# Sparse attention of a two-layer decoder trunk: the order of the attention slots' work

## The chip, the cores and the metric

One NeuronCore of a Trainium2 chip runs the whole kernel. The metric is the device time of one execution in microseconds (us). Three runs of the kernel before gave 2098.74, 2096.32 and 2098.92 us. The engines are TensorE (PE: matmuls; PEld: their weight loads), VectorE (DVE), ScalarE (ACT), GpSimd (POOL), and SyncE (SP), whose queue issues nearly all DMAs. Each engine takes its instructions in the order in which the program has them.

## What is computed

Two layers over 1024 tokens of width 1024: a gated linear attention layer, then a sparse attention layer, each with a projection, a residual layer norm and a gated addition. The change lies in the second layer, whose core is

```python
score = jnp.einsum('bths,bth->bts', rel, wi_b) * INDEX_SCALE      # indexer, causal
_, idx = lax.top_k(score, topk)                                   # 256 keys for each query
logits = jnp.einsum('bthd,btjd->bthj', q_b, k_sel) * ATTN_SCALE
probs = jax.nn.softmax(logits, axis=-1)
o = jnp.einsum('bthj,btjd->bthd', probs, v_sel)                   # 16 heads of 128
return (o * jax.nn.silu(z)) @ w_out
```

The kernel doesn't gather: it finds each query's threshold score, turns it into a bias that hides all other keys, and computes dense attention over the causal keys. All matmuls run on float32 split in a high and a low part, three matmuls for one.

## The kernel before

The second layer runs in two halves of 512 queries. Half 0 has up to 512 keys, half 1 up to 1024. X, the layer's input, lies in SBUF; q and the gate z of each head, and the output projection, are made by *units*: a unit is one 128-column weight block times X (24 matmuls of 512 columns), or half the output columns for a pair of heads (24 matmuls; one for two pairs has 48). `slots()` lists which units run in which slot. There are 17 slots in a half, h = -1 to 15.

In slot h the program places, between the matmuls of the units, the attention work of two heads (`attend`):

- the scores of head h+1 (`A`, four blocks t of 128 queries): matmuls into S, on DVE the bias and the row's limit (`L1371`, into P), on ACT the exponential (`exp`), on DVE the inverse of its sum (`inverse`), then `scaled`, which multiplies and writes into the one buffer sq (on POOL in half 0, on ACT in half 1), and `turned`, a transpose of 32x32 squares on DVE ("the turns");
- the stores of head h+1 (`store`): four DMAs from sq to DRAM for each 512 keys, so 4 in half 0 and 8 in half 1;
- the loads of the turned probabilities PT (`load`): one of 1 MB for each 512 keys. In half 0 it is issued in slot h+1, in half 1 the first (PT0) at the end of slot h and the second (PT1) in slot h+1. PT has two buffers in half 0, one in half 1 for each load;
- of head h, whose PT was loaded: `parts`, which splits PT into a copy ph (ACT) and the rest (a subtraction, on POOL in half 0 and DVE in half 1), 3 groups of keys in half 0 and 7 in half 1; and `pv`, the matmuls with v into o. The last pv is followed by the gate and the split into u, which the output units read.

The order is set while the program is written out. `Flow` keeps a clock that advances by each matmul's nominal time; `at(t, f)` and `after(dt, f)` put a step on a heap, and steps that are due are written between two groups of three matmuls. A step that raises NotReady (`req`) is tried again 0.3 later. So a step's number sets its place in each engine's row, not when it runs. `spread` places a list of steps evenly. `Weights` loads each unit's weight block (wst), makes its high part whi on ACT and its low part wlo on DVE; in half 0 the low parts of the second layer's blocks are stored (wlos) and in half 1 loaded. A `Background` writes one step of a generator every so many us: `topk_steps` (the thresholds of blocks 4 to 7, through half 0: it stores three score tiles, then sets their lowest bit in place, then finds the threshold bit by bit, counting on ACT and DVE), and the residual's transposes (slots 0 to 4).

Each unit of q is followed by its rotation (`rope`: a POOL multiplication, a DVE shuffle, multiplication and addition) and a split on ACT and DVE. After slot 15 come three more output units, then the tail (norm, gate). `load_p` in slot 15 loads two tiles of p (xst) for the tail and splits them into the buffers of q.

Of the kernel before, what the change touches and what calls it, by code (L numbers as in the profile page):

```python
# [11 lines left out]
F32R = mybir.dt.float32r  # L12
# [35 lines left out]
class Flow:  # L48
# [20 lines left out]
    def after(self, dt, fn):  # L69
        self.at(self.now + dt, fn)  # L70
# [155 lines left out]
def trunk_kernel(ctx, tc, x_tok, x_T, p_T, pos, freq, g_q, g_k, g_v, g_z, g_a, g_a2, g_ba, g_gn, g_o,  # L226
# [3 lines left out]
    fl = Flow(nc)  # L230
# [46 lines left out]
    def slots():  # L277


        yield [("z", 0), ("q", 1), ("z", 1)]  # L280
        z = 2
        for h in range(16):
            units = [("q", h + 2)] if h < 14 else []
            g = h // 4 - 1
            if g < 0 or h == 6:
                n = 1 + (h == 6)
            else:
                n = 0 if h % 4 < 2 and h < 14 else 2 if h < 15 else 0
            units += [("z", z + i) for i in range(n)]
            z += n  # L290
            if h < 14 and g >= 0 and h % 4 < 2:
                units.insert(h % 4 == 0, ("o", (2 * g, 2 * g + 1), h % 4))
            yield units + ([("o", (6,), 0)] if h == 15 else [])
        assert z == 16
# [443 lines left out]
                    u["out"] = (i + 1) // 4  # L738
                yield

    def load_p(layer, half, alloc):
        P = []
        for k in range(2):
            st = xp.tile([128, HT], F32, tag="xst", name="xst", bufs=2)
            nc.sync.dma_start(st, p_T[layer, k, :, half * HT:half * HT + HT])
            ph, pl = alloc(), alloc()
            after(3.0, lambda ph=ph, pl=pl, st=st: split(ph, pl, st))
            P.append((ph, pl))
        return P

# [238 lines left out]
    def topk_steps(Ts, scs, sp, junk, tmp, on_act=()):  # L989
# [32 lines left out]
        for i, j in enumerate(on_act):  # L1022
            n = scs[j].shape[1]
            nc.sync.dma_start(sc_s[i, :, :n], scs[j])
            dve.tensor_scalar(kr[:, j:j + 1], kr0[:, j:j + 1], 2.0, -float(n), op0=OP.mult, op1=OP.add)
            yield
            yield
            si = scs[j].bitcast(I32)
            dve.tensor_scalar(si, si, 1, None, op0=OP.bitwise_or)
            yield  # L1030
# [308 lines left out]
    def attend(st, h, half, ap, sq):  # L1339
# [14 lines left out]
        def A(t):  # L1354
            def f():
# [17 lines left out]
                    lim = mx  # L1373

                def scaled():
                    fl.req(st["x"] == nb * h, ("e", h, t) in st)
                    to, rows = by_key[:, t, :n // 128], P.rearrange("p (j b r) -> p j b r", b=4, r=32)
                    if half:
                        act.activation(to, rows, AF.Copy, scale=sm)  # L1379
                    else:  # L1380
                        pool.tensor_scalar(to, rows, sm, 0.0, op0=OP.mult, op1=OP.add)
                    st["P", h, t] = True
                    after(0.5 + n / 700.0, turned)

                def turned():
                    x = squares[:, t, :, :n // 128]
# [6 lines left out]

                def inverse():
                    dve.reciprocal(sm, sm)
                    st["e", h, t] = True
                after(0.9, exp)
                fl.at(max(fl.now + 1.8 + n / 1200.0, st["slot"] + 3.5 + (0.3 + n / 1000.0) * t), scaled)
            return f

        def store(i):
# [11 lines left out]
        def load(i):  # L1413

            def f():
                dt, = get(("dram", h, i))
                fl.req(st["pv"] >= (h * G - (0 if i else G - 4) if half else (h - 1) * G))
                PT = ap.tile([128, 4, HT], F32R, tag=f"PT{i}", name="PT", bufs=2 - half)
                nc.sync.dma_start(PT.bitcast(F32), dt.rearrange("b p a c -> (b p) a c"))
                st["PT", h, i] = PT  # L1420
            return f
# [79 lines left out]
    res, st = {}, {}  # L1501
# [44 lines left out]
    for half in range(NH):  # L1546
# [11 lines left out]
        for h, units in enumerate(plan, -1):  # L1558
            start = st["slot"] = fl.now
            dur = sum(len(u[1]) if u[0] == "o" else 1 for u in units) * B + core * (1.0 if h >= 0 else 0.5)  # L1560
            if h >= 0:
                _, parts, pvs, _, loads = S[h]
                fl.at(start + (1.5 if half else 0.8), loads[half])
                lead = 9.0 if half else 7.4
                spread(parts, start + lead, dur - lead - 2.4)
                spread(pvs, start + lead + 2.9, dur - lead - 2.4)
            if h < 15:
                first, _, _, stores, loads = S[h + 1]
                spread(first, start + 0.3, 5.8 if half else 4.4)
                for i, f in enumerate(stores):  # L1570
                    fl.at(start + (11.5 if half else 8.2) + 0.5 * i, f)
                if half:
                    fl.at(start + max(dur - 1.0, 18.0), loads[0])
            if h == 15:
                Pt = load_p(1, half, lambda: small_tile("q", F32R, 4))
            if h == -1:
                rows = x2_tiles(half)
                next(rows)
            elif h == 0:
                y = xp.tile([128, 4, D], F32, tag="y", name="y")  # L1580
                bg2.set(residual(y, rows), 4.6 if half else 3.3)
            elif h == 4:
                bg2.finish()
            fl.run(*(unit(u) for u in units))
# [82 lines left out]
```

## Time and profile before

| | us |
|---|---|
| median of three runs | 2098.74 |
| profiled execution | 2106.36 |
| its span, first to last instruction | 2104.1 |
| PE busy in it | 1998.5 |
| half 0 of the attention, first scores to slot 14 | 1104.7 to 1447.0 |
| half 1, first scores to slot 14 | 1578.5 to 1979.1 |

The mean granted clock of TensorE in the span was 0.984 of full speed. A slot is counted here from the first score matmul of a head to that of the next. The busy windows of the profile give for each stretch how long each engine was busy and the clock granted in it; the waits say which instruction an engine stood idle for, and what released it. What runs beside a busy PE costs nothing by itself.

### The profile page before, as it was taken

Reading aid. Unit: us, or ns where it says so; the run is one execution under the profiler, and the core shown is the slowest. Engines: PE = TensorE matmul, PEld = TensorE weight load, DVE = VectorE, ACT = ScalarE, POOL = GpSimd, SP = SyncE. Lnnn points to the kernel's source line nnn. Section 1 sums busy time; section 2 is a strip of 40 time slices with the busy share of each in tenths; the row PEclk is TensorE's granted clock in tenths of the full one; section 3 lists DMA queues with packets and bytes.
Section 4 is the critical chain, followed back from the end, with each engine's and each line's share of the span. In section 5 each row is a group of like instructions: output and inputs, shape, how many; then the busy total and the mean of one; then the engine's idle time right before and its main releaser. Section 6 shows DMA issues by size and latency. Waiting matters only on the chain.

```text
span 2104.1 us, 26226 instructions
## 1 busy us (share of the span) xinstructions
PE 1998.5 (95%) x8984; PEld 1622.8 (77%) x8984; DVE 1496.1 (71%) x3139; ACT 1153.6 (55%) x2105; POOL 258.6 (12%) x307
## 2 busy tenths in 40 slices
PE   8999999999999999999998999998799999999979
PEld 6788888888787888888876777777577777777767
DVE  5665565676867767668599887877886676767764
ACT  5563535354565353535466677766536666666623
POOL 0110000010002010001011343432100000000000
PEclk9999999999999999999999999999999999999989
DMA  4422222224431212122454887777457876868642
GB/s 143 161 81 82 81 82 80 81 86 145 146 121 53 99 66 97 64 97 81 150 175 131 256 254 237 229 222 228 159 185 254 271 253 232 300 236 303 243 143 92
DMA packets 108021, 336.37 MB, mean 160 GB/s; under 512 B 12656, under 2 KB 13296, under 8 KB 101744
## 3 DMA queue, kind: packets, MB, share of 16 engines
q1 hardware_dynamic: 107888, 334.71, 47.6%
q8 instruction: 70, 1.15, 0.2%
q14 instruction: 63, 0.52, 0.1%
HBM read 245.73 MB, written 88.93 MB: 159 GB/s over the span
## 4 chain that ended last, share of the span: by engine, by line
PE 65%; DVE 14%; ACT 8%; DMA 6%; issue 5%; POOL 1%; SPq 1%; DVEq 0%; POOLq 0%; ACTq 0%
PE pb L58 48%; PE o L58 7%; PE U L58 6%; DVE wlo L170 2%; PE S L58 2%; ACT sq L1379 2%; DVE P L1371 1%; DMA wlo<-wlos 1%; ACT P L1391 1%; DVE sq L1387 1%; DMA PT<-sqd 1%; DVE rt L867 1%; DVE sc L980 1%; DVE tk L1002 1%; SPq L1409 1%
## 5 line engine op out<-in xcount | busy, mean ns | idle before, releaser
L58 PE MATMUL pb<-x,whi 128*128 128x512 f32 x2272 | 713.9, 395 | 5.1 <-ACT whi L166 2.4
L58 PEld LDWEIGHTS pb<-x,whi 128*128 128x128 f32 x2272 | 421.4, 190 | 83.7 <-ACT whi L166 3.2
L58 PE MATMUL pb<-x,wlo 128*128 128x512 f32 x1136 | 446.4, 393 | 0.4 <-DVE wlo L170 0.3
L166 ACT ACTIVATE whi<-wst 128x512 fp32r<-128x512 f32 x556 | 327.2, 621 | 130.0 <-PE pb L58 31.3
L170 DVE TENSOR_TENSOR wlo<-wst,whi 128x512 fp32r<-128x512 f32 x460 | 317.0, 706 | 57.1 <-ACT whi L166 55.4
L58 PE MATMUL pb<-whi,u 128*128 128x512 f32 x1024 | 345.0, 397 | 7.1 <-DVE y L724 4.0
L58 PEld LDWEIGHTS pb<-x,wlo 128*128 128x128 f32 x1136 | 215.0, 189 | 49.1 <-DVE wlo L170 2.0
L58 PEld LDWEIGHTS pb<-whi,u 128*128 128x128 f32 x1024 | 194.8, 190 | 47.8 <-DVE y L724 4.4
L58 PE MATMUL pb<-wlo,u 128*128 128x512 f32 x512 | 202.2, 395 | 3.2 <-DMA wlo<-wlos 3.2
L58 PE MATMUL o<-ph,vT 128*128 128x512 f32 (+2 forms) x384 | 110.9, 375 | 18.1 <-ACT ph L1436 18.1
L1391 ACT ACTIVATE P<-P,ms 128x128 f32<-128x128 f32 (+7 forms) x128 | 98.6, 771 | 52.2 <-DVE ms L1371 44.4
L58 PE MATMUL S<-kT,q 128*128 128x512 f32 (+2 forms) x576 | 121.4, 343 | 3.1 <-DVE q L358 2.7
L1436 ACT ACTIVATE ph<-PT 128x512 fp32r<-128x512 f32 (+1 forms) x160 | 93.8, 599 | 44.4 <-DMA PT<-sqd 16.6
L58 PEld LDWEIGHTS S<-kT,q 128*128 128x128 f32 x576 | 100.5, 188 | 20.6 <-DVE q L358 3.7
L58 PEld LDWEIGHTS pb<-wlo,u 128*128 128x128 f32 x512 | 97.5, 190 | 21.9 <-DMA wlo<-wlos 3.6
L1387 DVE STREAM_TRANSPOSE sq<-sq 128x128 f32<-128x128 f32 (+7 forms) x128 | 97.1, 764 | 15.8 <-ACT sq L1379 12.3
L58 PE MATMUL o<-PT,vT 128*128 128x512 f32 x192 | 78.1, 407 | 31.5 <-POOL PT L1434 16.9
L675 ACT ACTIVATE junk<-o 128x512 bf16<-128x512 f32 x32 | 19.1, 597 | 161.2 <-DVE ot L673 151.8
L58 PEld LDWEIGHTS o<-ph,vT 128*128 128x128 f32 x384 | 74.8, 206 | 39.8 <-ACT ph L1436 27.2
L1044 ACT ACTIVATE tk<-sc,tki 128x768 f16<-128x768 f32 (+2 forms) x90 | 92.8, 1031 | 21.4 <-DVE tki L1053 20.6
L58 PE MATMUL pb<-whi,x 128*128 128x512 f32 x256 | 89.2, 408 | 9.5 <-ACT whi L166 6.2
L866 POOL TENSOR_TENSOR rt<-qf,tab 32x512 f32<-32x512 f32 x32 | 41.8, 1306 | 439.0 <-ACT qf L1288 433.1
(308 smaller groups left out, 3438.9 us busy)
## 6 DMA issues: line engine op xcount, KB each, us to landing
sqd<-sq SPq DMA_DIRECT2D x192, 256.0 KB, 4.5
PT<-sqd SPq DMA_DIRECT2D x48, 1024.0 KB, 7.8
wlos<-wlo SPq DMA_DIRECT2D x48, 512.0 KB, 7.0
wlo<-wlos SPq DMA_DIRECT2D x48, 512.0 KB, 7.7
wst<-in_g_v SPq DMA_DIRECT2D x32, 512.0 KB, 3.2
wst<-in_g_z SPq DMA_DIRECT2D x32, 512.0 KB, 3.3
wst<-in_g_o SPq DMA_DIRECT2D x32, 512.0 KB, 3.2
wst<-in_gate_c SPq DMA_DIRECT2D x32, 512.0 KB, 3.3
```

The source lines that it names most:

```text
L58: self.pe.matmul(out, lhsT, rhs, start=start, stop=stop)
L166: self.nc.scalar.activation(hi[:, c], st[:, c], AF.Copy)
L170: self.nc.vector.tensor_sub(lo[:, c], st[:, c], hi[:, c].bitcast(F32))
L866: pool.tensor_mul(b, x, c)
L867: dve.stream_shuffle(a, x, swap)
L980: dve.scalar_tensor_tensor(d, r[:, :e], w, d, op0=OP.mult, op1=OP.add)
L1002: dve.tensor_scalar(junk()[:, :n], scs[j], thr_ap, None, op0=op, op1=OP.add, accum_out=cnt[:, j:j + 1])
L1044: act.activation(junk()[:, :n], scs[j], AF.Sign, bias=cand[:, j:j + 1].bitcast(F32), accum_out=cnt[:, j:j + 1])
L1379: act.activation(to, rows, AF.Copy, scale=sm)
L1387: dve.transpose(x, x)
L1391: act.activation(P, P, AF.Exp, scale=-1.0, bias=mx, accum_out=sm)
L1436: chain((0, lambda: act.activation(hi, lo.bitcast(F32), AF.Copy)), (0.8, second))
```

## The change

`slots()`: slot -1 gets z's unit 2 as well (four units instead of three), slot 13 one unit less. q of head h+3, not h+2, is made in slot h, after z's units instead of ahead of them; slot 0 makes two. Slots 6, 10 and 14 keep their number of units.

In half 1 the first two `parts` get fixed times, 6.6 and 7.6 into the slot; the others keep theirs. `scaled` is put right behind `inverse`; before, it had a time of its own. `turned` follows it at a slightly smaller distance. A `load` needs both stores of its head to be written out, not only its own, and in slot -1 the first load has the time 16.0. In `load_p` of slot 15 the split of p comes 8.0 after the load instead of 3.0. In `topk_steps` the three stores are written first, three empty steps follow, then the three changes of the lowest bit.

```diff
@@ -277,18 +277,15 @@
     def slots():
 
 
-        yield [("z", 0), ("q", 1), ("z", 1)]
-        z = 2
+        yield [("z", 0), ("q", 1), ("z", 1), ("z", 2)]
+        z = 3
         for h in range(16):
-            units = [("q", h + 2)] if h < 14 else []
             g = h // 4 - 1
-            if g < 0 or h == 6:
-                n = 1 + (h == 6)
-            else:
-                n = 0 if h % 4 < 2 and h < 14 else 2 if h < 15 else 0
-            units += [("z", z + i) for i in range(n)]
+            n = 0 if h in (0, 15) else 1 if g < 0 else 0 if h % 4 < 2 else 2
+            units = [("z", z + i) for i in range(n)]
             z += n
-            if h < 14 and g >= 0 and h % 4 < 2:
+            units += [("q", i) for i in ((2, 3) if h == 0 else (h + 3,)) if i < 16]
+            if g >= 0 and h % 4 < 2:
                 units.insert(h % 4 == 0, ("o", (2 * g, 2 * g + 1), h % 4))
             yield units + ([("o", (6,), 0)] if h == 15 else [])
         assert z == 16
@@ -738,13 +735,13 @@
                     u["out"] = (i + 1) // 4
                 yield
 
-    def load_p(layer, half, alloc):
+    def load_p(layer, half, alloc, wait=3.0):
         P = []
         for k in range(2):
             st = xp.tile([128, HT], F32, tag="xst", name="xst", bufs=2)
             nc.sync.dma_start(st, p_T[layer, k, :, half * HT:half * HT + HT])
             ph, pl = alloc(), alloc()
-            after(3.0, lambda ph=ph, pl=pl, st=st: split(ph, pl, st))
+            after(wait, lambda ph=ph, pl=pl, st=st: split(ph, pl, st))
             P.append((ph, pl))
         return P
 
@@ -1024,7 +1021,9 @@
             nc.sync.dma_start(sc_s[i, :, :n], scs[j])
             dve.tensor_scalar(kr[:, j:j + 1], kr0[:, j:j + 1], 2.0, -float(n), op0=OP.mult, op1=OP.add)
             yield
-            yield
+        for _ in range(3 if on_act else 0):
+            yield
+        for j in on_act:
             si = scs[j].bitcast(I32)
             dve.tensor_scalar(si, si, 1, None, op0=OP.bitwise_or)
             yield
@@ -1373,14 +1372,14 @@
                     lim = mx
 
                 def scaled():
-                    fl.req(st["x"] == nb * h, ("e", h, t) in st)
+                    fl.req(st["x"] == nb * h)
                     to, rows = by_key[:, t, :n // 128], P.rearrange("p (j b r) -> p j b r", b=4, r=32)
                     if half:
                         act.activation(to, rows, AF.Copy, scale=sm)
                     else:
                         pool.tensor_scalar(to, rows, sm, 0.0, op0=OP.mult, op1=OP.add)
                     st["P", h, t] = True
-                    after(0.5 + n / 700.0, turned)
+                    after(0.4 + n / 1000.0, turned)
 
                 def turned():
                     x = squares[:, t, :, :n // 128]
@@ -1393,9 +1392,8 @@
 
                 def inverse():
                     dve.reciprocal(sm, sm)
-                    st["e", h, t] = True
+                    after(0.0, scaled)
                 after(0.9, exp)
-                fl.at(max(fl.now + 1.8 + n / 1200.0, st["slot"] + 3.5 + (0.3 + n / 1000.0) * t), scaled)
             return f
 
         def store(i):
@@ -1413,7 +1411,7 @@
         def load(i):
 
             def f():
-                dt, = get(("dram", h, i))
+                dt, _ = get(("dram", h, i), ("dram", h, nb - 1))
                 fl.req(st["pv"] >= (h * G - (0 if i else G - 4) if half else (h - 1) * G))
                 PT = ap.tile([128, 4, HT], F32R, tag=f"PT{i}", name="PT", bufs=2 - half)
                 nc.sync.dma_start(PT.bitcast(F32), dt.rearrange("b p a c -> (b p) a c"))
@@ -1562,7 +1560,11 @@
                 _, parts, pvs, _, loads = S[h]
                 fl.at(start + (1.5 if half else 0.8), loads[half])
                 lead = 9.0 if half else 7.4
-                spread(parts, start + lead, dur - lead - 2.4)
+                early = 2 * half
+                for i in range(early):
+                    fl.at(start + 6.6 + i, parts[i])
+                step = (dur - lead - 2.4) / len(parts)
+                spread(parts[early:], start + lead + early * step, dur - lead - 2.4 - early * step)
                 spread(pvs, start + lead + 2.9, dur - lead - 2.4)
             if h < 15:
                 first, _, _, stores, loads = S[h + 1]
@@ -1570,9 +1572,9 @@
                 for i, f in enumerate(stores):
                     fl.at(start + (11.5 if half else 8.2) + 0.5 * i, f)
                 if half:
-                    fl.at(start + max(dur - 1.0, 18.0), loads[0])
+                    fl.at(start + (max(dur - 1.0, 18.0) if h >= 0 else 16.0), loads[0])
             if h == 15:
-                Pt = load_p(1, half, lambda: small_tile("q", F32R, 4))
+                Pt = load_p(1, half, lambda: small_tile("q", F32R, 4), 8.0)
             if h == -1:
                 rows = x2_tiles(half)
                 next(rows)
```

What this makes of the instructions' order is shown at three places. First DVE in half 1, slot 1: head 1's parts (`PT<-PT,ph`) and head 2's turns (`STREAM_TRANSPOSE`, of 5, 6, 7 and 8 blocks of keys). Before:

```order
L1387 STREAM_TRANSPOSE sq<-sq 128x4x5x32
L1395 RECIPROCAL ms<-ms 128x1
L1387 STREAM_TRANSPOSE sq<-sq 128x4x6x32
L867 STREAM_SHUFFLE rt<-qf 32x512
L868 TENSOR_TENSOR rt<-rt,tab_8840 32x512
L1434 TENSOR_TENSOR PT<-PT,ph 128x4x128
L1387 STREAM_TRANSPOSE sq<-sq 128x4x7x32
L1387 STREAM_TRANSPOSE sq<-sq 128x32x32
L1434 TENSOR_TENSOR PT<-PT,ph 128x4x128
L871 TENSOR_TENSOR qf<-rt 32x512
L1434 TENSOR_TENSOR PT<-PT,ph 128x4x128 x3
```

And now:

```order
L1432 TENSOR_TENSOR PT<-PT,ph 128x4x128
L1386 STREAM_TRANSPOSE sq<-sq 128x4x5x32
L1394 RECIPROCAL ms<-ms 128x1
L1432 TENSOR_TENSOR PT<-PT,ph 128x4x128
L1386 STREAM_TRANSPOSE sq<-sq 128x4x6x32
L1394 RECIPROCAL ms<-ms 128x1
L1386 STREAM_TRANSPOSE sq<-sq 128x4x7x32
L1298 SCALAR_TENSOR_TENSOR z<-z,pb 128x512
L1386 STREAM_TRANSPOSE sq<-sq 128x32x32
L1432 TENSOR_TENSOR PT<-PT,ph 128x4x128 x3
```

The subtractions of parts 0 and 1 went ahead of the turns, the rotation (L867, L868, L871 before) left this place, and part 2 stays behind the last turn.

The same slot on ACT: exponentials (`P,ms<-P,ms`), scalings (`sq<-P,ms`), copies of the parts (`ph<-PT`). Before:

```order
L1379 ACTIVATE sq<-P,ms 128x5x4x32
L1379 ACTIVATE sq<-P,ms 128x6x4x32
L1391 ACTIVATE P,ms<-P,ms 128x1024
L1379 ACTIVATE sq<-P,ms 128x7x4x32
L1288 ACTIVATE qf<-pb 128x512
L1379 ACTIVATE sq<-P,ms 128x8x4x32
L1436 ACTIVATE ph<-PT 128x512
L166 ACTIVATE whi<-wst 128x512
L1436 ACTIVATE ph<-PT 128x512
L166 ACTIVATE whi<-wst 128x512
L1436 ACTIVATE ph<-PT 128x512 x3
```

And now:

```order
L1378 ACTIVATE sq<-P,ms 128x5x4x32
L1390 ACTIVATE P,ms<-P,ms 128x896
L1434 ACTIVATE ph<-PT 128x512
L1335 ACTIVATE y<-pb 128x4x128
L1434 ACTIVATE ph<-PT 128x512
L1390 ACTIVATE P,ms<-P,ms 128x1024
L1378 ACTIVATE sq<-P,ms 128x6x4x32
L1378 ACTIVATE sq<-P,ms 128x7x4x32
L1300 ACTIVATE z<-pb 128x512
L1378 ACTIVATE sq<-P,ms 128x8x4x32
L166 ACTIVATE whi<-wst 128x512 x2
L1434 ACTIVATE ph<-PT 128x512 x3
```

Two copies went ahead of the last exponential and three scalings; the third copy stands where it stood, behind the last scaling and two weight copies.

Third, SP at the end of half 1: the stores and loads of head 15, the tail's p (`xst`) and weights. Before:

```order
L745 DMA xst<-in_p_T 128x512 x2
L1409 DMA sqd<-sq 32x4x512 x4
L1419 DMA PT<-sqd 128x2048
L168 DMA wlo<-wlos 128x1024
L1409 DMA sqd<-sq 32x4x512 x4
L1419 DMA PT<-sqd 128x2048
L188 DMA wst<-in_ple_c 128x1024
```

And now:

```order
L1407 DMA sqd<-sq 32x4x512 x8
L1417 DMA PT<-sqd 128x2048
L742 DMA xst<-in_p_T 128x512 x2
L168 DMA wlo<-wlos 128x1024
L188 DMA wst<-in_ple_c 128x1024
L1417 DMA PT<-sqd 128x2048
```

All eight stores stand ahead of the first load, and four other DMAs now stand between the two loads.

## The prediction

> **What bounds the kernel.** I read the page first, then the busy windows, then the waits and the timelines of the attention stage.
>
> ```profile
> span 2104.1 us, 26226 instructions
> ```
>
> ```profile
> PE 1998.5 (95%) x8984; PEld 1622.8 (77%) x8984; DVE 1496.1 (71%) x3139; ACT 1153.6 (55%) x2105; POOL 258.6 (12%) x307
> ```
>
> TensorE is the bound: 95% busy, 0.222 us for each of 8984 matmuls. The change adds and removes none of them, so all that it can win or lose is idle time of PE and time at a reduced clock. I cut the attention stage at the first score matmul of a head (slot h runs from the scores of head h+1 to those of head h+2):
>
> ```profile
> 1141.30:1163.20 21.90, 17.48 (x81) 14.68 (x80) 21.55 (x52) 8.65 (x21) 7.95 (x8) 0.92 0.58 178
> 1163.20:1186.30 23.10, 18.86 (x82) 15.64 (x81) 16.70 (x46) 11.46 (x26) 8.98 (x8) 0.85 0.75 258
> 1186.30:1422.30 236.00, 222.01 (x1021) 180.23 (x1020) 192.69 (x499) 176.39 (x377) 90.44 (x88) 0.99 0.77 239
> 1447.00:1488.80 41.80, 33.02 (x124) 25.07 (x125) 28.38 (x67) 25.02 (x51) 9.95 (x10) 0.88 0.63 195
> 1595.10:1624.40 29.30, 24.36 (x106) 19.69 (x105) 18.15 (x42) 17.08 (x31) 1.28 (x1) 0.88 0.93 297
> 1624.40:1650.30 25.90, 23.48 (x105) 18.81 (x104) 18.24 (x43) 16.93 (x30) 1.28 (x1) 0.93 0.76 259
> 1650.30:1677.50 27.20, 24.76 (x106) 19.81 (x106) 18.54 (x43) 17.13 (x30) 1.29 (x1) 0.87 0.84 271
> 1677.50:1703.50 26.00, 23.59 (x98) 18.71 (x97) 17.88 (x39) 16.10 (x28) 1.28 (x1) 0.87 0.68 233
> 1948.70:1979.10 30.40, 30.28 (x140) 24.85 (x139) 20.45 (x46) 17.52 (x30) 1.29 (x1) 1.00 0.79 275
> 1979.10:2041.40 62.30, 50.16 (x200) 38.77 (x198) 38.48 (x78) 25.17 (x45) 2.14 (x4) 0.89 0.48 168
> ```
>
> Columns: length, busy time of PE, PEld, DVE, ACT, POOL, then PE's granted clock. A slot's loss is length minus PE busy, plus (1 - clock) times length. In half 0: slots 0 and 1 lose 6.2 and 7.7, slots 2 to 12 together 16 (14.0 idle), the end (from slot 14) 13.8. In half 1: slots 0 to 3 lose 8.5, 4.2, 6.0 and 5.8, slot 13 0.1, the end 19.0. That is some 70 us, and the change works there alone; layer 0 and the tails keep their order. A row of a timeline below gives start, duration, engine, line, operation, and in brackets how long the engine stood idle before it and what ended that.
>
> **Half 1, slots 1 to 3: the first two parts ahead of the turns.**
>
> ```profile
> 1637.52 0.73 PE L58 MATMUL o<-ph,vT 128*128 128x512 f32 x2 [0.44 <-ACT ph L1436]
> 1638.48 0.50 PE L58 MATMUL o<-PT,vT 128*128 128x512 f32 x1 [0.23 <-DVE PT L1434]
> 1638.81 0.63 PE L58 MATMUL o<-ph,vT 128*128 128x512 f32 x2
> 1641.20 0.50 PE L58 MATMUL o<-PT,vT 128*128 128x512 f32 x1 [1.75 <-DVE PT L1434]
> ```
>
> ```profile
> 1635.95 0.74 DVE L867 STREAM_SHUFFLE rt<-qf 32x512 f32<-32x512 f32 x1
> 1636.72 1.10 DVE L868 TENSOR_TENSOR rt<-rt,tab 32x512 f32<-32x512 f32 x1
> 1637.75 0.67 DVE L1434 TENSOR_TENSOR PT<-PT,ph 128x512 fp32r<-128x512 f32 x1
> 1638.35 2.22 DVE L1387 STREAM_TRANSPOSE sq<-sq 128x896 f32<-128x896 f32 x2
> 1640.51 0.64 DVE L1434 TENSOR_TENSOR PT<-PT,ph 128x512 fp32r<-128x512 f32 x1
> 1641.08 0.67 DVE L871 TENSOR_TENSOR qf<-rt 32x512 f32<-32x512 f32 x1
> ```
>
> ```profile
> 1638.93 1.14 ACT L1436 ACTIVATE ph<-PT 128x512 fp32r<-128x512 f32 x2
> ```
>
> PE waits 0.44 + 0.23 + 1.75 = 2.42 us, the last because the second part's subtraction stands behind two turns (2.22). Each part is a copy on ACT (L1436) and a subtraction on DVE (L1434). Moved ahead, parts 0 and 1 are ready and these waits go; the two subtractions cost DVE nothing new, they only trade places with the turns, and the turns end as late as the last scaling lets them. Next late is part 2, which stays behind all scalings on ACT. PE would be ready for part 0 at 1637.08 (1637.52 less 0.44); nine matmuls later, 2.0 us, it wants part 2 at 1639.1, and that copy starts at 1638.93 today. But q's unit now ends the slot, so its rotation and low part (0.74 + 1.10 + 0.67 and a subtraction of 0.67, 3.2 us) fall at the start of the next slot, ahead of the last score evictions on DVE. Part 2 slips by 0 to 3.2. I take a new wait of 2, near the 1.75 it replaces, and the same clock loss: **gain 1.5** for three slots. Bounds: -6 (waits of 2.9 and longer clock dips) to +15 (7.3 of idle and 8.7 of clock, less 1).
>
> The clock: in these slots it fell to 0.93, 0.87 and 0.87 with no wait above 1.8 us, so waits of this size cost clock too. [...]
>
> **The new wait on ACT.** The early copy needs the load of PT0:
>
> ```profile
> 1615.52 7.01 SPq L1409 DMA_DIRECT2D sqd<-sq  x8
> 1622.69 0.59 SPq L1419 DMA_DIRECT2D PT<-sqd  x1
> ```
>
> ```profile
> 1626.57 0.32 SPq L1419 DMA_DIRECT2D PT<-sqd  x1
> ```
>
> ```profile
> PT<-sqd SPq DMA_DIRECT2D x48, 1024.0 KB, 7.8
> ```
>
> Issued 7.2 after the first store and landed 7.8 later, at 1630.5, it is there 6.1 into the slot; the copy stands behind the exponential of block 2, later than that. If it waited, an exponential, three scalings, the second copy, an eviction and the last turn (eight instructions of 0.6 to 1.1, about 7) would wait behind it, and then the next stores: a loop of 7.2 + 7.8 + 7 = 22 a slot, below the 25.9 of today. So it costs nothing.
>
> **Half 1, slot 0.**
>
> ```profile
> 1604.53 0.83 ACT L1379 ACTIVATE sq<-P,ms 128x640 f32<-128x640 f32 x1 [5.09 <-issue]
> ```
>
> Scaling waited 5.09 for the stores of head 0 to leave sq. Slot -1 gets one more unit (24 matmuls, 5.3 us), which covers it. Slot 0 then loses what slots 1 to 3 lose on average, 5.3, for 8.5: **gain 3** (0 to 7). The earlier first load (16.0) hides behind the stores, which precede it on SP anyway.
>
> **Half 1, slots 4 to 12.**
>
> ```profile
> PE o L58 <- DVE PT L1434: 6.3, 7, 1.5
> ```
>
> All of PE's waits there are for those subtractions. Units stand between the parts, so part 2 is not late: **gain 4** (0 to 6.3). Scalings issued with the inverse sit on ACT at most 0.5 earlier; the rest of the slot covers that.
>
> **Half 1, slots 13 and end.** Slot 13 gives up a unit and becomes like slots 1 to 3, though without a rotation: **-1.5** (0 to -5.9). At the end:
>
> ```profile
> 2002.78 0.34 SPq L1419 DMA_DIRECT2D PT<-sqd  x1
> ```
>
> ```profile
> 2003.64 2.17 SPq L1409 DMA_DIRECT2D sqd<-sq  x4
> 2013.17 0.34 SPq L1419 DMA_DIRECT2D PT<-sqd  x1
> ```
>
> ```profile
> 2019.30 0.63 ACT L166 ACTIVATE whi<-wst 128x512 fp32r<-128x512 f32 x1 [9.19 <-DMA wst<-in_ple_c]
> ```
>
> ```profile
> 2020.50 0.80 PE L58 MATMUL o<-ph,vT 128*128 128x512 f32 x1 [5.65 <-ACT ph L1436]
> ```
>
> The first load held the second four stores back; with all eight ahead, the second load issues as in the slot above, 11.05 after the first store (1626.57 - 1615.52), not about 16.4. But four DMAs (1.5 MB, 5 to 6 us at the 0.26 to 0.3 MB/us of the windows) now stand between the loads. So 5.4 sooner less 0 to 5.5: I take **4** with the shorter clock dip (-1 to 9).
>
> **Half 0.** Top-k:
>
> ```profile
> 1175.60 0.63 DVE L1029 TENSOR_SCALAR sc<-sc 128x896 int32<-128x896 int32 x1 [4.96 <-DMA sc_s<-sc]
> ```
>
> DVE stood 4.96 for a store of top-k's scores; inverses, POOL's scaling and its subtraction queued behind. Six yields instead of two now lie between a store and its change, so the wait goes; slot 1 then loses 1.5, the mean of slots 2 to 12, for 7.7: **gain 6** (3 to 7). Slot 0 starts a unit later, so part of top-k's first counts fall ahead of it: **2** of 6.2 (-1 to 5; top-k's sign flips, which now meet the scores of head 1 on DVE, and its three stores, now close together on SP ahead of a load, are the risk).
>
> ```profile
> PE o L58 <- POOL PT L1434: 6.9, 12, 0.8
> ```
>
> In slots 2 to 12 the unit of q ends a slot in which it used to come first, so its rotation on POOL moves off the subtractions there: **3** (0 to 7). Slot 13 **-1.5** (0 to -3). End:
>
> ```profile
> 1468.12 1.27 ACT L366 ACTIVATE q<-xst 128x512 fp32r<-128x512 f32 x2 [3.94 <-DMA xst<-in_p_T]
> ```
>
> ```profile
> 1475.79 0.63 ACT L1436 ACTIVATE ph<-PT 128x512 fp32r<-128x512 f32 x1 [5.36 <-DMA PT<-sqd]
> ```
>
> ```profile
> 1471.57 0.67 PE L58 MATMUL pb<-whi,u 128*128 128x512 f32 x1 [3.97 <-DVE y L724]
> ```
>
> The split of p moves from 3.0 to 8.0 behind its load, so ACT's wait goes, and with it DVE's late addition and PE's 3.97; but the load of PT, which ends a wait of ACT 7 us further on, is late next, since it hangs on the scores' stores and not on p: **2** (0 to 6).
>
> **Sum.** 1.5 + 3 + 4 - 1.5 + 4 = 11 in half 1, 6 + 2 + 3 - 1.5 + 2 = 11.5 in half 0: 22.5 off. The profiled execution took 2106.4 (the span and 2.3 around it), so 2083.9; the runs' median is 7.6 lower and has the same waits: 2098.7 - 22.5 = **2076**.
>
> **Rivals.** (A) Forecast, 2076, chance 0.42. (B) Part 2 is in time: slots 1 to 3 give 13, not 1.5; 2065, 0.20. For it: 1638.93 is before 1639.1; against: the 3.2 us on DVE. (C) The wait in slots 1 to 3 stays, but as one piece of 2 it no longer lowers the clock, and 1.8 + 3.5 + 3.4 come back: 2076 - 8.7 = 2067, 0.08; three rows, with waits no longer than 1.75, are against it. [...] (D) The ends stay as long: the second load gains nothing (-1), slot 13 loses 5.9, half 0's end gives 0: 11.4 less, 2088, 0.13. (E) The moved waits come back one for one: about 2098, 0.08. (F) Slower: ACT stands at the early copy for PT0. It decides from a landing of some 14 us, where the loop is 28 a slot. At 15, the loop is 29.2 a slot: slots 0 to 3 grow by 8.4, 4 to 12 (27.2 each now) by 18, 13 by 4.3 over its 24.9; 30.7 less 4 and 11.5 still won is +15: 2114, 0.09. Against it: 7.8 and a DMA share of 0.68 to 0.93.
>
> **Range and chances.** Bounds of the terms together reach from -14 to +62; both ends at once are unlikely. 2050 to 2094 takes in A to D with their errors. This kernel is measured to about 0.2%, 4 us: faster 0.83 (A to D), same 0.08, slower 0.09.
>
> **What would show it.** Right: no wait for L1434 behind turns in half 1, a wait for the third part's copy in slots 1 to 3, no 4.96 and no 3.94, slot 0 of half 1 near 26. Wrong: slots 1 to 3 near 22 with a full clock (B), or a long ACT wait for PT ahead of an exponential (F).

## The result

The changed kernel takes **2064.05 us** (median of four runs, 2062.45 to 2071.66). The kernel before, four runs beside it, took 2098.83. The ratio is 0.9838, with a 95% interval of 0.9806 to 0.9870, so 34.8 us are gone where 22.5 were forecast. Four single executions in and beside the experiments (3264, 4578, 5637 and 6996 us; the profile of e11 is the first of them) lie far outside all others and are counted in no ratio. The profiled execution of the changed kernel took 2062.45. Its page begins:

```profile
span 2060.7 us, 26223 instructions
PE 1971.1 (96%) x8984; PEld 1612.2 (78%) x8984; DVE 1489.8 (72%) x3139; ACT 1151.2 (56%) x2105; POOL 257.0 (12%) x307
```

The same 8984 matmuls keep PE busy for 27.4 us less than before (1998.5): most of the gain is not idle time, but matmuls that run faster. By the granted clock (0.984 of 2104.1 before, 0.993 of 2060.7 now) some 19 of it is time at the reduced clock. The busy windows by stage (columns as in the prediction) show where. The changed kernel:

```profile
1143.50:1167.30 23.80, 18.84 (x82) 15.42 (x82) 20.96 (x53) 8.96 (x22) 9.51 (x9) 0.86 0.79 233
1167.30:1184.90 17.60, 16.50 (x82) 13.26 (x81) 14.06 (x39) 12.78 (x28) 9.91 (x9) 1.00 0.87 301
1184.90:1424.00 239.10, 222.66 (x1022) 181.27 (x1021) 192.12 (x505) 176.50 (x377) 87.73 (x88) 0.99 0.79 243
1438.90:1567.00 128.10, 115.16 (x501) 90.74 (x501) 113.33 (x208) 61.93 (x114) 21.11 (x20) 0.97 0.58 192
1589.00:1613.80 24.80, 23.25 (x105) 18.90 (x104) 17.27 (x42) 16.66 (x30) 2.53 (x2) 0.93 0.93 326
1613.80:1636.90 23.10, 21.70 (x106) 17.78 (x105) 17.76 (x43) 16.80 (x30) 1.30 (x2) 1.00 0.77 276
1636.90:1660.70 23.80, 21.59 (x106) 17.72 (x105) 17.71 (x43) 16.88 (x30) 1.26 (x2) 1.00 0.84 294
1660.70:1682.60 21.90, 20.44 (x99) 16.76 (x98) 16.53 (x37) 15.91 (x28) 1.12 (x2) 1.00 0.80 272
1682.60:1920.50 237.90, 232.54 (x1085) 194.11 (x1084) 175.30 (x406) 151.78 (x262) 11.78 (x10) 1.00 0.82 281
1940.40:2060.70 120.30, 107.50 (x492) 87.04 (x491) 74.43 (x138) 53.04 (x90) 4.99 (x8) 1.00 0.46 155
```

And the kernel before, for stretches that the prediction did not show whole (the end of half 0, slots 4 to 12 of half 1, the end of half 1):

```profile
1447.00:1578.50 131.50, 114.23 (x479) 88.26 (x480) 108.12 (x199) 61.32 (x112) 20.97 (x20) 0.96 0.52 174
1703.50:1948.70 245.20, 238.66 (x1085) 192.52 (x1084) 174.78 (x401) 152.42 (x261) 11.57 (x9) 1.00 0.79 270
1979.10:2104.10 125.00, 107.26 (x465) 85.89 (x463) 72.85 (x132) 51.27 (x87) 4.97 (x8) 0.94 0.38 131
```

In half 0, slot 1 is 5.5 shorter, but slot 0 and slots 2 to 12 are longer than before. In half 1, slots 1 to 3 run at the full clock, where they had 0.93, 0.87 and 0.87. Half 1 as a whole went from 525.6 to 493.7, half 0 from 473.8 to 465.2.

The table counts a segment's loss as the prediction did: idle time of PE plus half of the time at half clock, here from the trace's stretches, for both kernels and for the experiments below. An end runs from slot 14 to the next half or to the last matmul.

| loss, us | before | after | e1 | e2 | e3 | e5 | e12 | e10 | e7 |
|---|---|---|---|---|---|---|---|---|---|
| half 0: slot 0 | 6.1 | 8.4 | 8.4 | 6.2 | 8.6 | 6.9 | 4.9 | 5.0 | 7.4 |
| slot 1 | 7.6 | 1.1 | 0.8 | 7.8 | 0.6 | 1.4 | 4.2 | 0.8 | 1.3 |
| slots 4, 8, 12 | 4.3 | 15.1 | 16.4 | 6.7 | 4.3 | 4.3 | 11.5 | 13.7 | 5.5 |
| the other slots of 2 to 12 | 11.4 | 4.8 | 4.8 | 11.4 | 21.3 | 19.6 | 3.3 | 3.4 | 6.0 |
| end | 22.4 | 16.4 | 16.7 | 22.7 | 27.5 | 27.1 | 18.7 | 14.8 | 15.3 |
| half 1: slot 0 | 8.4 | 3.3 | 1.6 | 10.2 | 9.8 | 8.8 | 2.0 | 4.4 | 4.6 |
| slots 1 to 3 | 15.8 | 5.1 | 6.0 | 10.6 | 6.3 | 5.8 | 8.8 | 5.8 | 5.2 |
| slots 4 to 12 | 6.5 | 5.4 | 14.5 | 12.7 | 14.0 | 7.8 | 13.3 | 3.9 | 3.8 |
| end | 20.0 | 8.1 | 6.2 | 20.0 | 12.7 | 13.4 | 14.1 | 10.2 | 7.9 |

### The profile page after: what moved, and what is told of

The parts are those of the page before. It is cut to its first block, busy times and chain, and to the rows that moved or that the text cites. A ratio compares the mean times of both kernels' runs of the same rounds, so it can differ in the third digit from the quotient of the medians.

```text
span 2060.7 us, 26223 instructions
## 1 busy us (share of the span) xinstructions
PE 1971.1 (96%) x8984; PEld 1612.2 (78%) x8984; DVE 1489.8 (72%) x3139; ACT 1151.2 (56%) x2105; POOL 257.0 (12%) x307
## 4 chain that ended last, share of the span: by engine, by line
PE 68%; DVE 13%; ACT 7%; DMA 5%; issue 3%; POOL 2%; SPq 1%; POOLq 0%; DVEq 0%; ACTq 0%
PE pb L58 51%; PE o L58 6%; PE U L58 6%; PE S L58 2%; DMA PT<-sqd 2%; DVE wlo L170 2%; DVE P L1370 1%; ACT sq L1378 1%; DVE sq L1386 1%; POOL PT L1432 1%; DVE rt L864 1%; DVE sc L977 1%; ACT whi L166 1%; DMA sqd<-sq 1%; DMA wlos<-wlo 1%
## 5 line engine op out<-in xcount | busy, mean ns | idle before, releaser
L58 PE MATMUL o<-ph,vT 128*128 128x512 f32 (+2 forms) x384 | 103.1, 353 | 17.1 <-ACT ph L1434 17.1
L1043 ACT ACTIVATE tk<-sc,tki 128x768 f16<-128x768 f32 (+2 forms) x90 | 92.8, 1032 | 27.1 <-DVE tki L1052 25.5
L1434 ACT ACTIVATE ph<-PT 128x512 fp32r<-128x512 f32 (+1 forms) x160 | 92.7, 599 | 23.4 <-DMA PT<-sqd 12.4
L58 PEld LDWEIGHTS o<-ph,vT 128*128 128x128 f32 x384 | 69.7, 191 | 34.9 <-ACT ph L1434 23.5
L1432 DVE TENSOR_TENSOR PT<-PT,ph 128x512 fp32r<-128x512 f32 (+1 forms) x112 | 71.7, 662 | 24.8 <-ACT ph L1434 24.8
```

The source lines that it names most:

```text
L58: self.pe.matmul(out, lhsT, rhs, start=start, stop=stop)
L1043: act.activation(junk()[:, :n], scs[j], AF.Sign, bias=cand[:, j:j + 1].bitcast(F32), accum_out=cnt[:, j:j + 1])
L1432: (dve if half else pool).tensor_sub(lo, lo.bitcast(F32), hi.bitcast(F32))
L1434: chain((0, lambda: act.activation(hi, lo.bitcast(F32), AF.Copy)), (0.8, second))
```

## The experiments

Ratios are to the kernel before, measured beside each on the same chip, with a 95% interval; e6 was run once. The changed kernel's own is 0.9838 [0.9806, 0.9870], so differences from it of less than some 0.0035 can't be told from noise.

### The units and the early parts, apart and together

e1 is the changed kernel with `early = 0`; e2 the kernel before with only the early parts:

```diff
-                early = 2 * half
+                early = 0
```

> The changed kernel with the seven parts of half 1 spread as before (no fixed times for the first two). Theory 1, the early parts are what won in half 1: slots 1 to 3 of half 1, which lose 7.8 us now, lose 16 to 18 again, with PE waiting behind the turns for L1432 and a half-clock stretch of 3.4 or 6.8 us in most of them; slots 4 to 12 lose some 5 more; the time is 2064 + 13 to 16 = 2077 to 2080. Theory 2, the move of q's unit won it (its rotation is gone from among the turns): slots 1 to 3 stay below 11 in all, the time is within 4 of 2064.

> The kernel before with nothing but the fixed times of the first two parts in half 1. Theory 1: slots 1 to 3 of half 1 lose 8 to 11 instead of 18.1, slots 4 to 12 some 4 less, half 0 and the end stay: 2098.8 - 11 to 14 = 2085 to 2088. Theory 2: without the move of q's unit the rotation stands ahead of the third part, a new wait of the old size comes with its half clock, and the time stays within 4 of 2098.8.

e3 is the changed kernel with `slots()` of before, e5 the same with `early = 0`, e12 the kernel before with only the new `slots()`:

```diff
-        yield [("z", 0), ("q", 1), ("z", 1), ("z", 2)]
-        z = 3
+        yield [("z", 0), ("q", 1), ("z", 1)]
+        z = 2
...
-            units += [("q", i) for i in ((2, 3) if h == 0 else (h + 3,)) if i < 16]
+            units = [("q", h + 2)] if h < 14 else []
```

> The changed kernel with the units of each slot as before. Theory 1 (the order of the units costs in half 0 and pays only in slot 0 of half 1): slots 4, 8 and 12 of half 0 lose 2 each instead of 6.1, 4.8 and 7.3, so 12 less; slot 0 of half 1 loses 8 again instead of 4.1, slots 1 to 3 some 3 more: 2064 - 5 = 2059, at most 2064. Theory 2 (the order of the units is where half 1 won): slots 1 to 3 of half 1 lose 15 or more again, 2072 or above.

> The changed kernel with the units of each slot as before and without the early parts: what is left is the scaling issued with the inverse, the order of the loads, p's split and top-k's stores. It fills the square of four: both parts 2064 to 2069, units alone 2079, early parts alone 2101. If the two parts only help together (theory 3: each alone just moves the wait to another row), this kernel is within 5 of 2101, and slots 1 to 3 of half 1 lose 13 or more. If the early parts do harm where q's rotation stands ahead of the third part (theory 4), it is below 2095. If the two act apart from each other, it is 2101 + 13 = 2114.

> The kernel before with nothing but the new units of each slot. By the square of four the units took 19 off without the early parts (2098 to 2079), the rest 5. Theory 1, they win by themselves: 2103 - 19 = 2084, with half 0 losing some 12 less in slots 10, 11 and the end and some 9 more in slots 4, 8 and 12, and slot 0 of half 1 losing 3 to 4 instead of 8.6. Theory 2, they need the scaling issued with the inverse: above 2095.

| | ratio | interval |
|---|---|---|
| e2, before with only the early parts | 1.0022 | 1.0011 to 1.0032 |
| e12, before with only the new units | 0.9888 | 0.9871 to 0.9905 |
| e5, changed, old units, no early parts | 0.9974 | 0.9961 to 0.9987 |
| e3, changed, old units | 0.9984 | 0.9973 to 0.9996 |
| e1, changed, no early parts | 0.9883 | 0.9867 to 0.9898 |

The order of the units is the change: alone it gives 0.0112, some 23 us. The early parts by themselves cost 0.0022 (4.6 us); with the old units and the rest of the change they are worth nothing (0.9984 against 0.9974), with the new units 0.0045 (9.5 us, give or take 7.5). Theory 1 of e1 hit the time (2079.23 where 2077 to 2080 was expected) by luck, since the kernel before took 4 longer beside it: against that, 9.5 came back, not 13 to 16. It had the place wrong: slots 1 to 3 of half 1 hardly changed (6.0 against 5.1), it is slots 4 to 12 that lose 14.5 instead of 5.4. Of e2's two, theory 1 (2085 to 2088) fell, and the waits and half clock of theory 2 came back. Theory 2 of e3 had the direction (the time went back by 0.0146) and not the place: slots 1 to 3 stayed at 6.3. Theory 3 of e5 had the time, but not its 13 for slots 1 to 3, which lost 5.8. Theory 1 of e12 held (2079.93 against 2084).

Why they need each other stands in PE's waits in slots 4 to 12 of half 1 (total, times, longest). The kernel before had 6.3 for DVE's subtractions, as the prediction shows. e1, the changed kernel without the early parts:

```profile
PE o L58 <- DVE PT L1432: 6.7, 9, 1.4
PE o L58 <- ACT ph L1434: 3.4, 4, 0.9
```

e5, the old units without them, and then e3, the old units with them:

```profile
PE o L58 <- DVE PT L1435: 6.7, 10, 1.1
```

```profile
PE o L58 <- ACT ph L1437: 4.9, 4, 2.1
PE pb L58 <- DMA wlo<-wlos: 3.2, 1, 3.2
PE o L58 <- DVE PT L1435: 0.2, 1, 0.2
```

The changed kernel:

```profile
PE pb L58 <- DMA wlo<-wlos: 4.6, 3, 2.7
PE o L58 <- DVE PT L1432: 0.4, 1, 0.4
```

Early parts take the wait for the subtractions away in both (6.7 to 0.2 or 0.4), but on the old units a wait for a copy on ACT comes in its place. With the new units it does not. Which part of the new `slots()` does that (q one slot ahead, its place behind z, or the unit that moved to slot -1) was not tried apart.

What else the units do is seen at the ends. In the kernel before, q of the last head was made in slot 13's last unit, and the scores could only start when it was split. ACT and PE there, half 0:

```profile
1440.69 0.60 ACT L1288 ACTIVATE qf<-pb 128x512 f32<-128x512 f32 x1 [2.67 <-PE pb L58]
...
1446.35 0.63 ACT L366 ACTIVATE q<-qf 128x512 fp32r<-128x512 f32 x1 [2.37 <-DVE qf L871]
1447.04 0.50 PE L58 MATMUL S<-kT,q 128*128 128x256 f32 x2 [0.20 <-ACT q L366]
```

The unit's result is copied at 1440.69 and q is ready at 1446.98, so the scores came some 6 us after the last unit of slot 13, between the units of slot 14, and the stores, the load and everything behind them with it. In the changed kernel that q was split in slot 12:

```profile
1413.63 0.63 ACT L363 ACTIVATE q<-qf 128x512 fp32r<-128x512 f32 x1 [5.71 <-DVE qf L868]
...
1438.86 0.52 PE L58 MATMUL S<-kT,q 128*128 128x256 f32 x3
```

The scores start at 1438.86, between the first matmuls of slot 14. The last load of PT then issues 17.2 after the first score matmul (1456.05), where it was 19.9 (1466.95). With the old units the two ends lose 27.1 and 13.4 (e5), with the new ones 16.7 and 6.2 (e1); put into the kernel before, the new units take the ends from 22.4 and 20.0 to 18.7 and 14.1 (e12).

### Top-k's stores

```diff
             yield
-        for _ in range(3 if on_act else 0):
-            yield
-        for j in on_act:
+            yield
```

> The changed kernel with top-k's stores and bit changes in turn, as before. Theory 1: DVE stands some 5 for a store again in slot 1 of half 0, which loses 7 to 8 instead of 2.2: 2066 + 5 = 2071. Theory 2 (with the old units the loss only moved on, from 7.7 in slot 1 to 6.2 to 7.2 in slot 2): the time saved there is lost elsewhere, the time is within 2 of the changed kernel's.

Ratio 0.9840 [0.9820, 0.9860]: no difference from the changed kernel. DVE's rows in slot 1 of half 0:

```profile
1173.23 0.63 DVE L1026 TENSOR_SCALAR sc<-sc 128x896 int32<-128x896 int32 x1 [1.31 <-DMA sc_s<-sc]
1178.84 0.69 DVE L1026 TENSOR_SCALAR sc<-sc 128x1024 int32<-128x1024 int32 x1 [0.78 <-DMA sc_s<-sc]
```

With top-k as before and the new units, DVE comes to the bit changes only 1.31 and 0.78 ahead of the stores' landing, not 4.96. The slot loses 2.2, not 7.6. On the old units the new top-k frees slot 1 (7.6 to 1.4 in e5) and slot 2 loses 5.0 instead of 0.8. Theory 2 held for the time.

### The scaling behind the inverse

```diff
-                    fl.req(st["x"] == nb * h)
+                    fl.req(st["x"] == nb * h, ("e", h, t) in st)
...
-                    after(0.4 + n / 1000.0, turned)
+                    after(0.5 + n / 700.0, turned)
...
-                    after(0.0, scaled)
+                    st["e", h, t] = True
...
+                fl.at(max(fl.now + 1.8 + n / 1200.0, st["slot"] + 3.5 + (0.3 + n / 1000.0) * t), scaled)
```

> The changed kernel with the scalings and turns at their old times. The run with old units and without early parts lost 8.6 in slots 1 to 3 of half 1, the kernel before 18.1, so the scaling or the loads won there. Theory 1 (the earlier scalings bring the turns and the copies behind them forward, which the wait for the third part ends on): slots 1 to 3 wait 1 more each and fall under the half clock, +5 to +9, so 2071 to 2075. Theory 2 (the loads did it): no change, within 2 of 2066.

Both theories fell: the kernel is faster without this part of the change, 0.9794 [0.9779, 0.9809]; the interval just touches the changed kernel's. The loss of half 0 falls from 49.1 to 40.9, of which 6.4 is idle time; that of half 1 hardly moves (22.7 and 25.2). DVE's waits over the whole span, changed kernel and then e10:

```profile
DVE sq L1386 <- POOL sq L1380: 14.2, 25, 0.8
```

```profile
DVE sq L1386 <- POOL sq L1380: 3.1, 7, 0.6
```

A turn written right behind its scaling makes DVE stand for POOL, 25 times instead of 7, in the half in which DVE also counts for top-k; PE's waits for POOL's subtractions go from 16.2 in all to 11.2. The edit moves the scalings and the turns together, so which of the two costs the time is not shown apart.

### The loads and p

```diff
-                dt, _ = get(("dram", h, i), ("dram", h, nb - 1))
+                dt, = get(("dram", h, i))
...
-                    fl.at(start + (max(dur - 1.0, 18.0) if h >= 0 else 16.0), loads[0])
+                    fl.at(start + max(dur - 1.0, 18.0), loads[0])
...
-                Pt = load_p(1, half, lambda: small_tile("q", F32R, 4), 8.0)
+                Pt = load_p(1, half, lambda: small_tile("q", F32R, 4))
```

> The changed kernel with each load asking for its own store only, the first load of half 1 at its old time and p split 3.0 after its load. Theory 1 (the prediction's): half 0's end waits for p again, some 2 to 4 longer; in half 1 the first load goes ahead of the second four stores, the second load issues 5 later and the end loses 4 more; slots 1 to 3 the same: 2066 + 6 to 8 = 2072 to 2074. Theory 2: the first load is sooner there with its own store only, which is what ACT's early copy waits for in slots 1 to 3 (0.64 for PT0 in slot 2), so these lose less and the two cancel: 2064 to 2068.

Ratio 0.9870 [0.9853, 0.9888]: undoing it costs 0.0032, some 7 us, about what theory 1 had. But the interval overlaps the changed kernel's, so this price is likely, not shown; and as its profile is one of those four executions, where it is paid isn't shown at all.

### Waits of a known size

The copy of the fourth part of heads 5, 7, 9, 11 and 13 in half 1 is written 5 to 9 times:

```diff
+                more = {5: 4, 7: 5, 9: 6, 11: 7, 13: 8}.get(h, 0) if half and g == 3 else 0
...
-                chain((0, lambda: act.activation(hi, lo.bitcast(F32), AF.Copy)), (0.8, second))
+                chain((0, copies), (0.8, second))
```

> The changed kernel with the copy of the fourth part of heads 5, 7, 9, 11 and 13 in half 1 written 4, 5, 6, 7 and 8 times more (0.6 us each on ACT, the same values), in slots in which PE does not wait now. PE should wait some 0.5, 1.1, 1.7, 2.4 and 3.0 us in them. Theory of the 3.4 us windows: the half clock follows where the idle time inside one window (counted from the ends of the half-clock stretches of this run) is above about 1.6 to 1.9, so after the waits of about 2 and more unless a window's edge cuts them, and never after the two short ones. [...]

PE's waits, expected at 0.5, 1.1, 1.7, 2.4 and 3.0, came out at nothing (head 5), 1.69, 0.60, 3.00 and, in two pieces, 0.92 and 3.43. The windows of 3.4 us around the 1.69 and the 3.00:

```profile
1782.40:1785.80 3.40, 1.71 (x7) 0.81 (x6) 0.69 (x1) 3.31 (x6) 0.00 (x0) 1.00 1.01 346
1785.90:1789.30 3.40, 3.40 (x9) 2.63 (x9) 1.90 (x3) 1.48 (x4) 0.00 (x0) 0.50 0.94 276
1789.40:1792.70 3.30, 3.30 (x17) 2.80 (x16) 0.00 (x0) 0.28 (x1) 0.00 (x0) 1.00 0.97 263
1891.70:1895.10 3.40, 0.86 (x4) 0.38 (x2) 0.00 (x0) 3.24 (x6) 0.00 (x0) 1.00 0.97 345
1895.10:1898.50 3.40, 2.94 (x7) 2.32 (x8) 2.37 (x4) 2.90 (x6) 0.00 (x0) 0.50 0.91 280
```

A window with 1.69 idle is followed by one at 0.50, in which 9 matmuls run where the next one has 17; one with 2.54 of the 3.00 is followed by 0.50 too. Heads 5 and 9, with 0 and 0.60, were followed by none. For these four waits the theory held.

### Two mends and a third early part

e7 is the changed kernel with the second load of half 1 later, and the rotation of q later where q's unit is the first of its slot in half 0 (`wait` is 4.0 for head 2, 6.8 for heads 7, 11 and 15, else 0.8); e4 has only the last edit, e8 all three:

```diff
-                fl.at(start + (1.5 if half else 0.8), loads[half])
+                fl.at(start + (4.0 if half else 0.8), loads[half])
...
-        chain((0, lambda: None), (0.8, first), (1.6, second), (0.7, then))
+        chain((0, lambda: None), (wait, first), (1.6, second), (0.7, then))
...
-                early = 2 * half
+                early = 3 * half
```

> The changed kernel with the third part at a fixed time too, 8.6 into the slot. If the wait of PE for the third part's copy (1.40, 2.21 and 1.46 us in slots 1 to 3 of half 1) is an end of its own, it goes: 5 less idle, 2064 - 5 = 2059. Rival: the third copy and subtraction now delay the scalings and turns, and with them the stores and the next head's first load, or PE waits for the fourth part in its place: 2064 or up to 4 above.

> The changed kernel with the second load of half 1 at 4.0 in the slot instead of 1.5, so that the low parts of the output units' weights go ahead of it on SP, and with the rotation of q in half 0 later by 6.0 (3.2 in slot 0) where q's unit is the first of its slot, so that POOL takes the subtractions ahead of it. If PE's waits for wlo (2.68, 1.27 and 0.70 in slots 4, 8 and 12 of half 1) come from the load ahead of them, they go: -5 with their drained weight loads. If ACT stands for q's rotation in slots 4, 8 and 12 of half 0, these lose 2 each instead of 6.1, 4.8 and 7.3, and slot 0 loses 4 instead of 8.4: -12 to -16. Together 2066 - 15 to 20 = 2046 to 2051. Rival for half 0: POOL's work is the limit whatever its order, the loss stays: 2061. Rival for half 1: the later PT1 makes its parts late, +5 there.

> The same with the third part early too. With the weights no longer late, the third early part can show its gain in slots 1 to 3 of half 1 (3 to 5 less idle): 2 to 4 below the run with two early parts. If what it delays on ACT counts more, it is the same or slower.

e7: 0.9796 [0.9777, 0.9816], a gain of 0.0042, 9 us, where 15 to 20 were expected. PE's waits for the weights' low parts, changed kernel and then e7:

```profile
PE pb L58 <- DMA wlo<-wlos: 6.2, 4, 2.7
```

```profile
PE pb L58 <- DMA wlo<-wlos: 0.6, 1, 0.6
```

Slots 4, 8 and 12 of half 0 lose 5.5 instead of 15.1: in slot 12 ACT had stood 5.71 for q's rotation (the row at 1413.63 above), with the copy that PE wanted behind it, and PE's wait of 3.31 for that copy is now 0.51; in slot 8 it went from 1.56 to nothing, in slot 4 it stayed (1.94 and 1.95). Slot 0 gained 1.0 where 4 were expected. The third early part wins nothing: 0.9849 in e4, where slots 1 to 3 of half 1 lose 3.2 instead of 5.1 but slots 4 to 12 12.2 instead of 5.4, as the rival had it, and 0.9817 in e8, where e7 without it had 0.9796. e7 and e10 have the lowest ratios of all; they mend different things and were not run together.

## Why the prediction was right, and where it was wrong

The forecast of 2076 was 12 too high, and its direction held: the matmuls are the same, and idle time and clock were saved. Of its signs, the waits for the third part, the end of the 4.96 and the 3.94, and a shorter slot 0 of half 1 (24.8, 26 forecast) came; of PE's 14.0 of waits for subtractions in half 1, 2.0 are left. The terms, with the loss before and after from the table (slots 4 to 12 of half 1 by their length):

| term | forecast | in the profiles |
|---|---|---|
| half 1, slots 1 to 3 | 1.5 | 10.7 |
| half 1, slot 0 | 3 | 5.1 |
| half 1, slots 4 to 12 | 4 | 7.3 |
| half 1, end | 4 | 11.9 |
| half 0, slot 1 | 6 | 6.5 |
| half 0, slot 0 | 2 | -2.3 |
| half 0, slots 2 to 12 | 3 | -4.2 |
| half 0, end | 2 | 6.0 |
| slot 13 of both halves | -3 | -1.1 |

The two profiled executions lie further apart (43.9) than the medians (34.8), so these terms sum to more than the result: 39.9. They miss the forecast's terms by -7.2 to +9.2, the misses add up to +28.9 and -11.5, and that the time came out within the range owes something to their cancelling. Part of the 43.9 is luck too: of the 3.41 us windows (cut as in the last section) with 1.5 to 2.0 of idle time, 6 of 7 were followed by half clock in the profile before and 2 of 7 in the other, a difference of 4 windows or some 7 us. The losses that the prediction lists add up to 87, not to "some 70"; its sum doesn't use that figure.

**Half 1, slots 1 to 3: the wait as forecast, the clock mis-sized.** The forecast had a new wait of 2 for the third part. It came, with 1.40, 2.21 and 1.46. That q's rotation makes it, as the forecast had it, is not shown: in e3, where the rotation stands where it stood, PE waits 1.6 to 2.5 for the same part. The longest:

```profile
1653.78 0.73 PE L58 MATMUL o<-ph,vT 128*128 128x512 f32 x2 [2.21 <-ACT ph L1434]
```

The step that failed is "the same clock loss". Of the 10.7, 8.5 is clock: before, three waits within some 4 us put 1.6 to 1.8 of idle time into one window each time, and the clock fell each time; now it did not fall once, though the wait of 2.21 put 1.93 into one window. This was luck. In e6, the same up to slot 4, the wait of slot 2 is 2.2 again, and there the clock does fall (a loss of 3.9 for 2.2). In e2, with waits of 2.4 in all three slots as before, it fell in two. So the 8.7 of the three rows was one execution's price of such waits, not a fixed one; rival C, at 0.08, was nearest, though not for its reason. The timed runs, whose mean granted clock lay at 0.982 to 0.989 before and 0.989 to 0.993 now, vary with it: 2062.45 at 0.993, 2071.66 at 0.989.

**Half 1, slots 4 to 12: a cost that idle time doesn't show.** Idle time and clock fell by 1.1 only. PE's busy time for the same 1085 matmuls fell by 6.1 (238.66 to 232.54). A part's three matmuls, before:

```profile
1772.43 0.73 PE L58 MATMUL o<-ph,vT 128*128 128x512 f32 x2
1773.16 0.50 PE L58 MATMUL o<-PT,vT 128*128 128x512 f32 x1
1773.49 0.62 PE L58 MATMUL pb<-x,whi 128*128 128x512 f32 x2
```

And in the changed kernel:

```profile
1749.35 0.62 PE L58 MATMUL o<-ph,vT 128*128 128x512 f32 x2
1749.80 0.39 PE L58 MATMUL o<-PT,vT 128*128 128x512 f32 x1
1750.03 0.62 PE L58 MATMUL pb<-x,whi 128*128 128x512 f32 x2
```

From the part's first matmul to the one behind it, 1.06 before and 0.68 now, with no idle time shown in PE's rows of either. The weight loads show it: before, they stood 0.38 for the copy and 0.43 for the subtraction.

```profile
1772.43 0.30 PEld L58 LDWEIGHTS o<-ph,vT 128*128 128x128 f32 x2 [0.38 <-ACT ph L1436]
1773.16 0.19 PEld L58 LDWEIGHTS o<-PT,vT 128*128 128x128 f32 x1 [0.43 <-DVE PT L1434]
```

Their waits for the subtractions in slots 4 to 12, before and then now (total, times, longest):

```profile
PEld o L58 <- DVE PT L1434: 16.5, 24, 2.0
```

```profile
PEld o L58 <- DVE PT L1432: 2.6, 6, 0.8
```

The forecast counted only the 6.3 of PE's own waits.

**What the new units are worth.** The prediction gave them 3 in slot 0 of half 1, 2 and 3 in half 0 and minus 1.5 twice; they are worth some 23. Slot 0 of half 1 went as argued (8.8 to 1.6 from e5 to e1). Missed was that q one slot ahead lets the last scores start with slot 14 (the ends: 10.4 and 7.2 from e5 to e1), and that the early parts' value hangs on the units. The ends were put down to the loads and p alone; e11 prices these at some 7 together, about the 6 forecast, within the noise named there. Of the 11.9 at the end of half 1, 7 is clock: no half-clock stretch fell there in the changed kernel's profile, two in e9's.

**Half 0, slot 1: the right size, but not top-k's to claim.** The 4.96 is gone and the slot gained what was forecast. On the old units the new order of top-k does free it (1.4 in e5), but slot 2 then loses 5.0 instead of 0.8; the new units free it with the old top-k too (2.2 in e9, 4.2 in e12). In this kernel top-k's new order is worth nothing that the runs can show.

**Half 0, slots 0 and 2 to 12: the sign was wrong.** Two steps failed. The scaling behind the inverse was costed on ACT of half 1 only ("at most 0.5 earlier"); in half 0 it makes DVE stand for POOL, and e10, without it, loses 8 less there. And q's rotation was moved "off the subtractions" in most slots (11.4 to 4.8), but in slots 4, 8 and 12 q is still the first unit, and these went from 4.3 to 15.1, which e7 brings down to 5.5.

**Rival F** had ACT stand at the early copy, and the forecast said that the loop of stores and loads is shorter than a slot, "so it costs nothing". ACT did stand, in slot 2 of half 1, for PT0, which was there 9.2 into the slot and not 6.1:

```profile
1646.13 0.63 ACT L1434 ACTIVATE ph<-PT 128x512 fp32r<-128x512 f32 x1 [0.64 <-DMA PT<-sqd]
```

```profile
1630.33 7.32 SPq L1407 DMA_DIRECT2D sqd<-sq  x8
1637.97 0.99 SPq L1417 DMA_DIRECT2D PT<-sqd  x1
1653.68 7.21 SPq L1407 DMA_DIRECT2D sqd<-sq  x8
```

From one head's first store to the next head's the loop took 23.4 there, not 22, and the slot takes 23.8: with the shorter slots it is as long as one. PE's wait for the third part is some 0.8 longer in this slot (2.21) than in slots 1 and 3 (1.40 and 1.46). That the 0.64 makes it so is likely and was not tried apart. The growth of all slots that F feared did not come.

## What to carry to other kernels

Where several steps of a hand-written order move together, price them in pairs: a step taken out of a queue gains only if the next operand on that path is early too, and here one part was worth -5 us alone and some +9 beside the other. Ask first which operand the slot's first work waits for; in the last slot of each half, having it one slot ahead moved the stores and loads behind it. Where the idle time in a 3.41 us window came to 1.5 to 2.0, half clock followed in 8 of 14 cases here (see the next section): price a wait that brings it there with and without a half-clock stretch, and not by what one execution happened to pay.

## What the runs showed of the hardware

**Half clock after idle time.** In the profile before, 15 stretches have a granted clock of 0.50, in the changed kernel's 8. Each is 3.41 or 6.83 us long (the last of each profile 3.40 and 3.00), and in each profile all begin at one phase of a 3.41 us grid. Both spans were cut into windows on that grid, from 700 us on. A window at full clock with under 1.5 us of idle time was followed by a half-clock window in 0 of 757 cases, with 1.5 to 2.0 in 8 of 14, with 2.0 or more in 11 of 11. A window at half clock was followed by another in 0 of 19 cases when it had under 0.5 idle, and in 6 of 6 when it had more (0.64 to 2.63). Idle time here is the trace's, whose matmul ends are modelled, which may be why 1.5 to 2.0 went both ways. The wait of 2.21 lay in two windows, 1.93 of it in the first, and the granted clock was 1.00 in both. A half-clock window is priced here at 1.7, an estimate: half of its 3.41, by the granted 0.50.

**Parts whose operand came just in time took 0.2 to 0.4 longer on PE,** with no idle time shown in PE's rows, as above: of the parts of 512 columns in slots 4 to 12 with no wait of PE, 15 of 36 took 0.89 to 1.06 before instead of 0.68, and 1 of 42 more than 0.71 now.

**DVE beside POOL.** In slot 0 of half 0, while POOL ran the rotation and three subtractions, two subtractions on DVE took 3.72 together:

```profile
1157.78 3.72 DVE L170 TENSOR_TENSOR wlo<-wst,whi 128x512 fp32r<-128x512 f32 x2
```

The mean of one is 0.715 over the kernel. In the changed kernel's trace the 384 of them with no POOL instruction beside took 0.64 to 0.69; of the 41 beside a POOL multiplication or subtraction (TENSOR_TENSOR), 14 took 1.1 to 2.7, these two among them. Whether POOL's work slows them, and what in it, was not tried apart.
